# Seven-product pairs: the third output sum behind the last product, the low part behind a weight sum, and a fifth ordinary pair at the head of each module

## The chip, the cores and the metric

The kernel runs on one core of one Trainium2 chip. The metric is the device time of one execution in microseconds (us), the median of several runs. Engines are named as in the profile: PE (TensorE, matmuls), PEld (its weight loads), DVE (VectorE), ACT (ScalarE), POOL (GpSimd), SP (the queue that issues most transfers).

## What is computed

The reference is a trunk of two layers on 512 tokens of width 1024. Each layer is a mixer (a convolution module in layer 0, a chunked gated DeltaNet in layer 1) between two half-step feed-forward modules, with a shift, scale and gate from a conditioning vector. The change concerns the feed-forward modules of layer 1 alone:

```
gate, up = split(h @ w_in, 2)             # 1024 -> 2 x 2816
y = (silu(gate) * up) @ w_out             # 2816 -> 1024
x = x + 0.5 * (1 + mod) * y
```

## The kernel before, in words

All products are made of float32 values split into a high and a low part, and each product is three matmuls: high by high, high by low, low by high (`mm3`, lines 175 to 177, and the copy of it in `seven`, lines 661 to 663). The activations lie as feature tiles by 512 tokens: `hh` and `hl` for the input h, `ahi` and `alo` for silu(gate) * up.

`ffn` (line 501 on) handles the 2816 hidden features as 22 pairs; a pair is 128 features of gate and the same 128 of up. The pairs come in three groups of 7, 7 and 8 (`GROUPS`). After a group, its part of the second matrix product is added to x in eight parts of 128 output features, one block each. Below, a module is one of these feed-forward modules, of which layer 1 has two, and a block is one call of `block`.

An **ordinary pair** is two calls of `block`: 8 chunks of 128 input features, times three matmuls of 512 columns, for gate and again for up. Before them the raw weights are loaded (`raw`, three buffers), copied to the high part on ACT (`whi`) and subtracted on DVE (`wlo`): a weight split, made by `feed.prep`. Afterwards come `glu_a` (silu of gate, ACT), `glu_b` (times up, DVE line 552), and `glu_c` (the copy ahi on ACT, and alo on DVE).

A **seven-product pair** (`seven`) computes the same with seven products of half-size operands in place of eight, in the manner of Strassen: input features and tokens are cut in two, and each product is 4 chunks times three matmuls of 256 columns, 84 matmuls in all. It needs sums of the activations, `th` and `tl`, made once per module in four tasks (`sums_h`, with two additions on POOL, line 565, and six operations on DVE, lines 568 to 575), and sums of each pair's weights, made while the pair ahead of it runs (`sums_w`, four parts):

- `first`: s1 on POOL (line 594) from the raw up weights.
- `second`: the copy gh on ACT, s2 on DVE (line 602), the remainder gl on DVE, two copies of sums on ACT.
- `third`: s3 on POOL (line 612), a copy on ACT, s4 on DVE (line 617), three remainders on DVE (line 583), two copies on ACT.
- `fourth`: two remainders on DVE (line 583), and the next two raw loads.

The seven products go to three PSUM tiles Y, X and Z of one bank each. Products 0, 2, 4 and 6 add up in the left half of Y, products 1 and 5 in the left half of X, product 3 goes to the left half of Z. In between, ACT copies what has been summed so far: p1 after product 0 (line 674), p5 after product 1, u2 after product 2, u3 after product 4 (line 684). DVE makes three output sums from them: the left half of Z (line 680), the right half of Y from u3 and p5 (line 685), and the right half of Z (line 688). Then Z holds gate, and Y holds up. The silu is issued at the end of the pair; the product, ahi and alo are kept back in the list `late`, and `settle` issues them behind product 0 of the next pair.

`LEAD` says how many ordinary pairs stand at the head of a module, while the activation sums are made: four. In this head, `side` is a list of tasks of which each `block` issues one: the three remaining tasks of `sums_h`, then the four parts of the first `sums_w` in two tasks. Three of the first four outputs are begun by the stage ahead, so four ordinary pairs have five calls of `block`.

All of it stands under a manual schedule: each engine works off its instructions in the order in which the program issues them, and semaphores make an instruction wait for the tiles that it reads or overwrites. Two engines on one PSUM bank are kept apart in the same way.

Of the kernel before, what the change touches and what calls it, by code (L numbers as in the profile page):

```python
# [48 lines left out]
ARB = 3  # L49
PAD = (40, 168)  # L50
KQ = KT // 2
LEAD = {(1, 0): 4, (1, 1): 4}
SNW = 7
XP = ((0, 1), (1, 1), (2, 2), (4, 2), (6, 2))
WARM = (4, 7, 4)
# [54 lines left out]
def trunk_kernel(ctx: ExitStack, tc: tile.TileContext, x_in, c_in, vecs, consts, w_ada, w_st,  # L110
# [390 lines left out]
    def ffn(layer, which, nxt, first=None):  # L501
# [4 lines left out]
        with tc.tile_pool(name=nm("ffn"), bufs=1) as ap, ExitStack() as ax:  # L506
# [19 lines left out]
            box = {}  # L526
# [25 lines left out]
                dve.tensor_tensor(pr, box["s"], u, ALU.mult)  # L552

            def glu_c(jj):
                pr = box["pr"]
                act.copy(ahi[:, jj, :], pr)  # L556
                dve.tensor_tensor(alo[:, jj, :], pr, ahi[:, jj, :].bitcast(F32), ALU.subtract)  # L557

            def sums_h(th, tl):
                def task(k):  # L560
# [18 lines left out]
            def sums_w(box):  # L579
                st = {}  # L580

                def low(dst, src, hi):
                    dve.tensor_tensor(dst, src, hi.bitcast(F32), ALU.subtract)  # L583
# [12 lines left out]
                def second():  # L596
                    g, s1 = st["g"], st["s1"]
                    gh = wp.tile([P, KT, P], F32R, tag="whi", name=nm("whi"))
                    gl = wp.tile([P, KT, P], F32R, tag="wlo", name=nm("wlo"))
                    act.copy(gh, g)  # L600
                    st["s2"] = s2 = raw_s("sq")
                    dve.tensor_tensor(s2, s1, g[:, :KQ, :], ALU.subtract)
                    low(gl, g, gh)
                    st["h1"] = h1 = fresh("shi")
                    act.copy(h1[:, 0], s1)
                    act.copy(h1[:, 1], s2)
                    st["gw"] = gh, gl
# [34 lines left out]
            late = []  # L642

            def settle():
                while late:
                    late.pop(0)()

            def seven(w, th, tl, jj, prep):
                l, r = halves
                lo4, hi4 = slice(0, KQ), slice(KQ, KT)  # L650

                def T_(i):
                    return th[:, i], tl[:, i]

                def H_(ks, sl):
                    return hh[:, ks, sl], hl[:, ks, sl]

                def prod(i, ps, m, ends):
                    (whi, wlo), (mhi, mlo) = w[i], m
                    for k in range(KQ):  # L660
                        pe.matmul(ps, whi[:, k, :], mhi[:, k, :], start=ends in (0, 2) and k == 0, stop=False, skip_group_check=True)  # L661
                        pe.matmul(ps, whi[:, k, :], mlo[:, k, :], start=False, stop=False, skip_group_check=True)  # L662
                        pe.matmul(ps, wlo[:, k, :], mhi[:, k, :], start=False, stop=ends in (2, 3) and k == KQ - 1, skip_group_check=True)  # L663

                Y, X, Z = mm_tile(), mm_tile(), mm_tile()
                y, e = Y[:, l], X[:, l]
                pp = scratch("ssum").rearrange("p (a n) -> p a n", a=2)
                uu = scratch("t", bufs=2).rearrange("p (a n) -> p a n", a=2)
                p1, p5, u2, u3 = pp[:, 0], pp[:, 1], uu[:, 0], uu[:, 1]
                prod(0, y, H_(lo4, l), 0)  # L670
                settle()
                prep[0]()
                prod(1, e, T_(0), 0)
                act.copy(p1, y)
                prep[1]()
                prod(2, y, T_(1), 1)
                act.copy(p5, e)
                prod(3, Z[:, l], H_(hi4, l), 2)
                act.copy(u2, y)  # L679
                dve.tensor_tensor(Z[:, l], Z[:, l], p1, ALU.add)  # L680
                prep[2]()
                prod(4, y, T_(2), 1)
                prod(5, e, H_(hi4, r), 3)
                act.copy(u3, y)
                dve.tensor_tensor(Y[:, r], u3, p5, ALU.add)
                prep[3]()
                prod(6, y, T_(3), 3)
                dve.tensor_tensor(Z[:, r], e, u2, ALU.add)
                glu_a(Z)

                def rest():
                    glu_b(Y)
                    glu_c(jj)

                late.append(rest)

            def no():
                pass
# [1 line left out]
            for gi, n in enumerate(GROUPS):  # L700
                ahi = ap.tile([P, n, T], F32R, tag="ahi", name=nm("ahi"))
                alo = ap.tile([P, n, T], F32R, tag="alo", name=nm("alo"))
                if gi == 0 and lead < NPAIR:
                    th = ap.tile([P, 4, KQ, H2], F32R, tag="th", name=nm("th"))
                    tl = ap.tile([P, 4, KQ, H2], F32R, tag="tl", name=nm("tl"))
                    side += sums_h(th, tl)
                    side.pop(0)()
                    nxw = {}
                    s4 = sums_w(nxw)
                    side += [lambda: (s4[0](), s4[1]()), lambda: (s4[2](), s4[3]())]  # L710
                for jj in range(n):
                    if starts[gi] + jj >= lead:
                        w, nxw = nxw["w"], {}
                        if jj < n - 1:
                            prep = sums_w(nxw)
                        else:
                            prep = (no, feed.prep, feed.prep, feed.prep)
                        seven(w, th, tl, jj, prep)
                        continue
                    if len(begun) > 1:  # L720
# [7 lines left out]
                        step(rate[1])  # L728
                    glu_b(u)
                    glu_c(jj)  # L730
                settle()

                if gi == ng - 1:
# [1229 lines left out]
```

## Time and profile before

| | |
|---|---|
| runs shown | 2060.54, 2062.14, 2063.51 us (median 2062.14) |
| profiled execution, its own time | 2059.63 us |
| its span in the profile | 2057.8 us |
| busy: PE, PEld, DVE, ACT, POOL | 96%, 83%, 67%, 44%, 15% of the span |
| mean granted clock of TensorE | 0.984 |

The profile is of one execution. A row of the timeline gives start, length, engine, line of the kernel, operation, tiles written and read, and in brackets how long the engine had been idle and what ended that. A matmul's length includes its pass through the array, so the distance of two starts tells how long one occupies PE.

### The profile page before, as it was taken

Reading aid. Unit: us, or ns where it says so; the run is one execution under the profiler, and the core shown is the slowest. Engines: PE = TensorE matmul, PEld = TensorE weight load, DVE = VectorE, ACT = ScalarE, POOL = GpSimd, SP = SyncE. Lnnn points to the kernel's source line nnn. Section 1 sums busy time; section 2 is a strip of 40 time slices with the busy share of each in tenths; the row PEclk is TensorE's granted clock in tenths of the full one; section 3 lists DMA queues with packets and bytes.
Section 4 is the critical chain, followed back from the end, with each engine's and each line's share of the span. In section 5 each row is a group of like instructions: output and inputs, shape, how many; then the busy total and the mean of one; then the engine's idle time right before and its main releaser. Section 6 shows DMA issues by size and latency. Waiting matters only on the chain.

```text
span 2057.8 us, 29707 instructions
## 1 busy us (share of the span) xinstructions
PE 1982.2 (96%) x11651; PEld 1718.2 (83%) x11651; DVE 1373.2 (67%) x2190; ACT 904.7 (44%) x1660; POOL 317.5 (15%) x228
## 2 busy tenths in 40 slices
PE   8999999998899999999899999999899998999998
PEld 6888888877898888889889899887677897898997
DVE  7767676799865556546857576676745668475674
ACT  6422222564642222224535354476656545353452
POOL 0000000399100000001202020024210103021110
PEclk9999999999899999999999999999899999999999
DMA  8767776222235666532233333322111222333231
GB/s 301 236 226 236 229 235 225 98 82 84 90 117 188 209 190 208 162 95 72 81 101 96 103 95 122 110 77 72 62 54 41 64 91 81 94 103 113 83 113 62
DMA packets 78495, 262.29 MB, mean 127 GB/s; under 512 B 8337, under 2 KB 14097, under 8 KB 78226
## 3 DMA queue, kind: packets, MB, share of 16 engines
q1 hardware_dynamic: 77810, 259.87, 39.6%
q8 instruction: 91, 1.49, 0.3%
q10 hardware_dynamic: 544, 0.52, 0.1%
q14 instruction: 50, 0.41, 0.1%
HBM read 254.59 MB, written 5.77 MB: 127 GB/s over the span
## 4 chain that ended last, share of the span: by engine, by line
PE 77%; DVE 11%; ACT 4%; issue 4%; POOL 3%; DMA 1%; SPq 0%; DVEq 0%; POOLq 0%; ACTq 0%
PE mm L175 19%; PE mm L176 19%; PE mm L177 19%; PE mm L661 5%; PE mm L663 4%; PE mm L662 4%; POOL pacc L849 3%; DVE slo L583 2%; DVE sq L617 1%; DVE wlo L583 1%; PE mm L1616 1%; DVE x L1358 1%; PE mm L1638 1%; PE mm L1624 1%; PE aux L380 1%
## 5 line engine op out<-in xcount | busy, mean ns | idle before, releaser
L175 PE MATMUL mm<-hh,whi 128*128 128x512 f32 (+1 forms) x1392 | 518.9, 374 | 6.2 <-ACT hh L276 4.4
L176 PE MATMUL mm<-hl,whi 128*128 128x512 f32 (+1 forms) x1392 | 513.1, 369 | 1.6 <-DVE hl L280 1.3
L177 PE MATMUL mm<-hh,wlo 128*128 128x512 f32 (+1 forms) x1392 | 511.2, 368 | 1.8 <-DVE wlo L167 1.8
L167 DVE TENSOR_TENSOR wlo<-raw,whi 128x1024 fp32r<-128x1024 f32 (+1 forms) x219 | 267.8, 1224 | 156.3 <-ACT whi L166 152.1
L166 ACT CAST whi<-raw 128x1024 fp32r<-128x1024 f32 (+1 forms) x219 | 221.8, 1014 | 220.2 <-PE mm L176 195.3
L175 PEld LDWEIGHTS mm<-hh,whi 128*128 128x128 f32 x1392 | 263.4, 190 | 51.9 <-ACT hh L276 5.5
L177 PEld LDWEIGHTS mm<-hh,wlo 128*128 128x128 f32 x1392 | 264.2, 190 | 46.3 <-DVE wlo L167 2.9
L176 PEld LDWEIGHTS mm<-hl,whi 128*128 128x128 f32 x1392 | 264.4, 190 | 45.1 <-DVE hl L280 3.7
L175 PE MATMUL mm<-ahi,whi 128*128 128x512 f32 (+1 forms) x768 | 286.2, 373 | 0.0
L176 PE MATMUL mm<-alo,whi 128*128 128x512 f32 (+1 forms) x768 | 285.6, 372 | 0.0
L177 PE MATMUL mm<-ahi,wlo 128*128 128x512 f32 (+1 forms) x768 | 285.5, 372 | 0.0
L176 PEld LDWEIGHTS mm<-alo,whi 128*128 128x128 f32 x768 | 144.8, 189 | 24.9
L177 PEld LDWEIGHTS mm<-ahi,wlo 128*128 128x128 f32 x768 | 144.7, 188 | 24.9
L175 PEld LDWEIGHTS mm<-ahi,whi 128*128 128x128 f32 x768 | 144.7, 188 | 24.7
L429 DVE CUSTOM_DVE_ANT_0 ajunk<-araw,cs 128x1024 bf16<-128x1024 f32 x128 | 156.1, 1220 | 0.6
L556 ACT CAST ahi<-t 128x512 fp32r<-128x512 f32 x88 | 54.7, 622 | 223.7 <-DVE t L552 223.7
L548 ACT ACTIVATE sil<-mm 128x512 f32<-128x512 f32 x88 | 52.6, 598 | 214.3 <-PE mm L177 121.8
L473 DVE SCALAR_TENSOR_TENSOR x<-mm,gate,x 128x512 f32<-128x512 f32 x64 | 48.1, 751 | 122.8 <-PE mm L177 122.8
L661 PE MATMUL mm<-th,shi 128*128 128x256 f32 x432 | 124.3, 288 | 1.5 <-ACT t L679 1.3
L662 PE MATMUL mm<-tl,shi 128*128 128x256 f32 x432 | 123.7, 286 | 0.0
L663 PE MATMUL mm<-th,slo 128*128 128x256 f32 x432 | 123.6, 286 | 0.0
L557 DVE TENSOR_TENSOR alo<-t,ahi 128x512 fp32r<-128x512 f32 x88 | 76.9, 873 | 60.5 <-ACT ahi L556 60.5
(317 smaller groups left out, 3566.3 us busy)
## 6 DMA issues: line engine op xcount, KB each, us to landing
raw<-in_w_fi_dram SPq DMA_DIRECT2D x169, 512.0 KB, 3.6
araw<-in_w_ada_dram SPq DMA_DIRECT2D x128, 512.0 KB, 4.5
raw<-in_w_fo_dram SPq DMA_DIRECT2D x64, 448.0 KB, 3.4
raw<-in_w_dn_dram SPq DMA_DIRECT2D x33, 512.0 KB, 3.3
raw<-in_w_fo_dram SPq DMA_DIRECT2D x32, 512.0 KB, 3.6
stage<-in_w_ada_dram SPq DMA_DIRECT2D x16, 512.0 KB, 6.5
raw<-in_w_glu_dram SPq DMA_DIRECT2D x16, 512.0 KB, 3.6
raw<-in_w_pw_dram SPq DMA_DIRECT2D x8, 512.0 KB, 3.3
```

What stands on the lines that cost most here:

```text
L166: act.copy(whi[:, :nk, :], raw[:, :nk, :])
L167: dve.tensor_tensor(wlo[:, :nk, :], raw[:, :nk, :], whi[:, :nk, :].bitcast(F32), ALU.subtract)
L175: pe.matmul(ps, whi[:, k, :], mhi, start=first, stop=False)
L176: pe.matmul(ps, whi[:, k, :], mlo, start=False, stop=False)
L177: pe.matmul(ps, wlo[:, k, :], mhi, start=False, stop=last)
L429: dve.tensor_tensor_reduce(junk, raw, ada["cs"], 1.0, 0.0, ALU.mult, ALU.add, accum_out=mod[:, layer, col:col + 1])
L557: dve.tensor_tensor(alo[:, jj, :], pr, ahi[:, jj, :].bitcast(F32), ALU.subtract)
L583: dve.tensor_tensor(dst, src, hi.bitcast(F32), ALU.subtract)
L661: pe.matmul(ps, whi[:, k, :], mhi[:, k, :], start=ends in (0, 2) and k == 0, stop=False, skip_group_check=True)
L662: pe.matmul(ps, whi[:, k, :], mlo[:, k, :], start=False, stop=False, skip_group_check=True)
L663: pe.matmul(ps, wlo[:, k, :], mhi[:, k, :], start=False, stop=ends in (2, 3) and k == KQ - 1, skip_group_check=True)
L849: pool.tensor_tensor(pacc[m][:, c], pacc[m][:, c], pr[:, c], ALU.add)
```

## The change

It has four parts. The output sum of line 685 (right half of Y) is no longer issued between products 5 and 6 but with the product of silu and up, in `rest`, which `settle` issues behind product 0 of the next pair. The list `late` now has two entries per pair, and `settle` issues one at a time: alo, now `glu_d`, comes out behind the weight sum s2 of the next pair, or in the last pair of a group ahead of a weight split. Two scratch tiles are allocated after `settle` in place of before it. And `LEAD` is five, so pair 4 of each of the two modules is an ordinary pair; at the head, the four parts of the first `sums_w` are spread over four calls of `block`, the first of which issues none.

```diff
@@ -49,7 +49,7 @@
 ARB = 3
 PAD = (40, 168)
 KQ = KT // 2
-LEAD = {(1, 0): 4, (1, 1): 4}
+LEAD = {(1, 0): 5, (1, 1): 5}
 SNW = 7
 XP = ((0, 1), (1, 1), (2, 2), (4, 2), (6, 2))
 WARM = (4, 7, 4)
@@ -552,9 +552,10 @@
                 dve.tensor_tensor(pr, box["s"], u, ALU.mult)
 
             def glu_c(jj):
-                pr = box["pr"]
-                act.copy(ahi[:, jj, :], pr)
-                dve.tensor_tensor(alo[:, jj, :], pr, ahi[:, jj, :].bitcast(F32), ALU.subtract)
+                act.copy(ahi[:, jj, :], box["pr"])
+
+            def glu_d(jj):
+                dve.tensor_tensor(alo[:, jj, :], box["pr"], ahi[:, jj, :].bitcast(F32), ALU.subtract)
 
             def sums_h(th, tl):
                 def task(k):
@@ -600,6 +601,7 @@
                     act.copy(gh, g)
                     st["s2"] = s2 = raw_s("sq")
                     dve.tensor_tensor(s2, s1, g[:, :KQ, :], ALU.subtract)
+                    settle()
                     low(gl, g, gh)
                     st["h1"] = h1 = fresh("shi")
                     act.copy(h1[:, 0], s1)
@@ -642,7 +644,7 @@
             late = []
 
             def settle():
-                while late:
+                if late:
                     late.pop(0)()
 
             def seven(w, th, tl, jj, prep):
@@ -664,12 +666,12 @@
 
                 Y, X, Z = mm_tile(), mm_tile(), mm_tile()
                 y, e = Y[:, l], X[:, l]
+                prod(0, y, H_(lo4, l), 0)
+                settle()
+                prep[0]()
                 pp = scratch("ssum").rearrange("p (a n) -> p a n", a=2)
                 uu = scratch("t", bufs=2).rearrange("p (a n) -> p a n", a=2)
                 p1, p5, u2, u3 = pp[:, 0], pp[:, 1], uu[:, 0], uu[:, 1]
-                prod(0, y, H_(lo4, l), 0)
-                settle()
-                prep[0]()
                 prod(1, e, T_(0), 0)
                 act.copy(p1, y)
                 prep[1]()
@@ -682,17 +684,17 @@
                 prod(4, y, T_(2), 1)
                 prod(5, e, H_(hi4, r), 3)
                 act.copy(u3, y)
-                dve.tensor_tensor(Y[:, r], u3, p5, ALU.add)
                 prep[3]()
                 prod(6, y, T_(3), 3)
                 dve.tensor_tensor(Z[:, r], e, u2, ALU.add)
                 glu_a(Z)
 
                 def rest():
+                    dve.tensor_tensor(Y[:, r], u3, p5, ALU.add)
                     glu_b(Y)
                     glu_c(jj)
 
-                late.append(rest)
+                late.extend((rest, lambda: glu_d(jj)))
 
             def no():
                 pass
@@ -707,14 +709,14 @@
                     side.pop(0)()
                     nxw = {}
                     s4 = sums_w(nxw)
-                    side += [lambda: (s4[0](), s4[1]()), lambda: (s4[2](), s4[3]())]
+                    side += [no, lambda: (s4[0](), s4[1]()), s4[2], s4[3]]
                 for jj in range(n):
                     if starts[gi] + jj >= lead:
                         w, nxw = nxw["w"], {}
                         if jj < n - 1:
                             prep = sums_w(nxw)
                         else:
-                            prep = (no, feed.prep, feed.prep, feed.prep)
+                            prep = (no, lambda: (settle(), feed.prep()), feed.prep, feed.prep)
                         seven(w, th, tl, jj, prep)
                         continue
                     if len(begun) > 1:
@@ -728,6 +730,8 @@
                         step(rate[1])
                     glu_b(u)
                     glu_c(jj)
+                    glu_d(jj)
+                settle()
                 settle()
 
                 if gi == ng - 1:
```

What moves on the engines is shown at three places. First DVE, through one seven-product pair of the second group, from the left half of Z on (names: mm are the PSUM tiles, t holds u2 and u3 or the gate product, ssum p1 and p5, pr s1 or s3, sq s2 or s4, slo and wlo remainders). Before:

```order
L680 TENSOR_TENSOR mm_8669<-mm_8669,ssum_8670 128x256
L617 TENSOR_TENSOR sq_8744<-raw_8532,sq_8706 128x512
L583 TENSOR_TENSOR slo_8746<-pr_8688,shi_8709 128x512
L583 TENSOR_TENSOR slo_8746<-sq_8706,shi_8709 128x512
L583 TENSOR_TENSOR wlo_8742<-raw_8648,whi_8741 128x512
L685 TENSOR_TENSOR mm_8667<-t_8671,ssum_8670 128x256
L583 TENSOR_TENSOR slo_8779<-pr_8739,shi_8750 128x512
L583 TENSOR_TENSOR slo_8779<-sq_8744,shi_8750 128x512
L688 TENSOR_TENSOR mm_8669<-mm_8668,t_8671 128x256
L552 TENSOR_TENSOR t_8818<-sil_8799,mm_8667 128x512
L557 TENSOR_TENSOR alo_8536<-t_8818,ahi_8535 128x512
L602 TENSOR_TENSOR sq_8840<-pr_8822,raw_8650 128x512
```

In the changed kernel:

```order
L682 TENSOR_TENSOR mm_8602<-mm_8602,ssum_8621 128x256
L619 TENSOR_TENSOR sq_8678<-raw_8466,sq_8639 128x512
L584 TENSOR_TENSOR slo_8680<-pr_8619,shi_8643 128x512
L584 TENSOR_TENSOR slo_8680<-sq_8639,shi_8643 128x512
L584 TENSOR_TENSOR wlo_8676<-raw_8581,whi_8675 128x512
L584 TENSOR_TENSOR slo_8712<-pr_8673,shi_8684 128x512
L584 TENSOR_TENSOR slo_8712<-sq_8678,shi_8684 128x512
L689 TENSOR_TENSOR mm_8602<-mm_8601,t_8622 128x256
L693 TENSOR_TENSOR mm_8600<-t_8622,ssum_8621 128x256
L552 TENSOR_TENSOR t_8750<-sil_8732,mm_8600 128x512
L603 TENSOR_TENSOR sq_8773<-pr_8753,raw_8583 128x512
L558 TENSOR_TENSOR alo_8470<-t_8750,ahi_8469 128x512
```

The right half of Y (L685, now L693) went from between the remainders to behind the right half of Z, and alo went behind s2 (L602, now L603).

Second DVE at the head of the first module of layer 1, from the last remainder of the activation sums on. Before:

```order
L575 TENSOR_TENSOR tl_7651<-pr_7796,th_7650 128x2x256
L552 TENSOR_TENSOR t_7809<-sil_7768,mm_7770 128x512
L557 TENSOR_TENSOR alo_7649<-t_7809,ahi_7648 128x512
L602 TENSOR_TENSOR sq_7843<-pr_7838,raw_7646 128x512
L583 TENSOR_TENSOR wlo_7841<-raw_7646,whi_7840 128x1024
L617 TENSOR_TENSOR sq_7881<-raw_7646,sq_7843 128x512
L583 TENSOR_TENSOR slo_7883<-pr_7838,shi_7846 128x512
L583 TENSOR_TENSOR slo_7883<-sq_7843,shi_7846 128x512
L583 TENSOR_TENSOR wlo_7879<-raw_7678,whi_7878 128x512
L583 TENSOR_TENSOR slo_7890<-pr_7876,shi_7887 128x512
L583 TENSOR_TENSOR slo_7890<-sq_7881,shi_7887 128x512
```

In the changed kernel:

```order
L576 TENSOR_TENSOR tl_7651<-pr_7802,th_7650 128x2x256
L552 TENSOR_TENSOR t_7815<-sil_7768,mm_7776 128x512
L558 TENSOR_TENSOR alo_7649<-t_7815,ahi_7648 128x512
L167 TENSOR_TENSOR wlo_7820<-raw_7678,whi_7819 128x1024
L603 TENSOR_TENSOR sq_7882<-pr_7877,raw_7727 128x512
L584 TENSOR_TENSOR wlo_7880<-raw_7727,whi_7879 128x1024
L552 TENSOR_TENSOR t_7888<-sil_7850,mm_7852 128x512
L558 TENSOR_TENSOR alo_7649<-t_7888,ahi_7648 128x512
L619 TENSOR_TENSOR sq_7922<-raw_7727,sq_7882 128x512
L584 TENSOR_TENSOR slo_7924<-pr_7877,shi_7885 128x512
L584 TENSOR_TENSOR slo_7924<-sq_7882,shi_7885 128x512
L584 TENSOR_TENSOR wlo_7920<-raw_7774,whi_7919 128x512
```

One more weight split (L167) stands here, and another gate product with its alo has come between the weight sums of the first seven-product pair.

Third ACT at the same head, at the start of the first seven-product pair. Before:

```order
L623 CAST shi_7887<-pr_7876 128x512
L624 CAST shi_7887<-sq_7881 128x512
L556 CAST ahi_7648<-t_7897 128x512
L674 COPY ssum_7904<-mm_7901 128x256
L600 CAST whi_7933<-raw_7727 128x1024
L605 CAST shi_7939<-pr_7918 128x512
```

In the changed kernel:

```order
L617 CAST whi_7919<-raw_7774 128x512
L625 CAST shi_7928<-pr_7917 128x512
L626 CAST shi_7928<-sq_7922 128x512
L548 ACTIVATE sil_7931<-mm_7892 128x512
L555 CAST ahi_7648<-t_7965 128x512
L676 COPY ssum_7986<-mm_7969 128x256
L601 CAST whi_8001<-raw_7823 128x1024
```

The copy ahi of the last ordinary pair stands ahead of p1 (ssum) in both; a silu has come before it.

## Rows read from the trace of the kernel before

**Rows 1.** What PE waited for, whole span: total us, times, longest us.

```profile
PE mm L661 <- DVE mm L685: 10.9, 28, 0.4
...
PE mm L661 <- ACT whi L600: 5.4, 2, 2.7
...
PE mm L663 <- DVE wlo L583: 3.9, 2, 1.9
```

**Rows 2.** Timeline of PE, pairs 20 and 21 (the last of 0 to 21): start us, length, engine, line, tiles.

```profile
1247.89 0.28 PE L661 MATMUL mm<-hh,whi 128*128 128x256 f32 x1
...
1256.41 0.28 PE L663 MATMUL mm<-hh,slo 128*128 128x256 f32 x1
1257.08 0.39 PE L661 MATMUL mm<-th,whi 128*128 128x256 f32 x1 [0.39 <-DVE mm L685]
...
1258.61 0.28 PE L661 MATMUL mm<-hh,whi 128*128 128x256 f32 x1
...
1268.69 0.40 PE L175 MATMUL mm<-ahi,whi 128*128 128x512 f32 x1
```

**Rows 3.** Timeline of DVE in pair 20, one row for each step spoken of.

```profile
1247.41 0.42 DVE L688 TENSOR_TENSOR mm<-mm,t 128x256 f32<-128x256 f32 x1
1248.50 0.69 DVE L552 TENSOR_TENSOR t<-sil,mm 128x512 f32<-128x512 f32 x1 [0.66 <-ACT sil L548]
1249.88 1.14 DVE L557 TENSOR_TENSOR alo<-t,ahi 128x512 fp32r<-128x512 f32 x1 [0.69 <-ACT ahi L556]
...
1251.54 1.21 DVE L583 TENSOR_TENSOR wlo<-raw,whi 128x1024 fp32r<-128x1024 f32 x1
1253.85 0.43 DVE L680 TENSOR_TENSOR mm<-mm,ssum 128x256 f32<-128x256 f32 x1 [1.10 <-PE mm L663]
1254.19 0.68 DVE L617 TENSOR_TENSOR sq<-raw,sq 128x512 f32<-128x512 f32 x1
1254.79 0.69 DVE L583 TENSOR_TENSOR slo<-pr,shi 128x512 fp32r<-128x512 f32 x1
...
1256.60 0.43 DVE L685 TENSOR_TENSOR mm<-t,ssum 128x256 f32<-128x256 f32 x1
...
1258.14 0.43 DVE L688 TENSOR_TENSOR mm<-mm,t 128x256 f32<-128x256 f32 x1
```

**Rows 4.** Timeline of ACT in pair 20: ahi, p1 and u3.

```profile
1249.22 0.62 ACT L556 CAST ahi<-t 128x512 fp32r<-128x512 f32 x1 [0.75 <-DVE t L552]
1249.75 0.36 ACT L674 COPY ssum<-mm 128x256 f32<-128x256 f32 x1
...
1255.44 0.37 ACT L684 COPY t<-mm 128x256 f32<-128x256 f32 x1
```

**Rows 5.** Timeline of POOL in pair 20: s1 and s3.

```profile
1247.91 1.29 POOL L594 TENSOR_TENSOR pr<-raw 128x512 f32<-128x512 f32 x1 [8.03 <-DVE mm L688]
1249.16 1.30 POOL L612 TENSOR_TENSOR pr<-raw,raw 128x512 f32<-128x512 f32 x1
```

**Rows 6.** The page's row of weight loads: engine, operation, times, KB, median us to landing.

```profile
raw<-in_w_fi_dram SPq DMA_DIRECT2D x169, 512.0 KB, 3.6
```

**Rows 7.** Timeline of PE at the head of the first module.

```profile
987.67 0.39 PE L175 MATMUL mm<-hh,whi 128*128 128x512 f32 x1
...
992.88 0.39 PE L177 MATMUL mm<-hh,wlo 128*128 128x512 f32 x1
995.95 0.39 PE L661 MATMUL mm<-hh,whi 128*128 128x256 f32 x1 [2.68 <-ACT whi L600]
...
1012.15 0.28 PE L661 MATMUL mm<-hh,whi 128*128 128x256 f32 x1
```

**Rows 8.** Timeline of DVE at the same head: fourth activation sum, pair 2's product.

```profile
990.64 0.41 DVE L568 TENSOR_TENSOR pr<-sq 128x256 f32<-128x256 f32 x1
...
993.62 0.68 DVE L552 TENSOR_TENSOR t<-sil,mm 128x512 f32<-128x512 f32 x1
```

**Rows 9.** Two stretches: length, busy PE, PEld, DVE, ACT, POOL, granted clock, DMA.

```profile
990.00:1000.00 10.00, 5.38 (x24) 4.28 (x23) 9.05 (x14) 5.89 (x10) 3.04 (x3) 0.85 0.00 0
...
1435.00:1445.00 10.00, 8.64 (x41) 6.90 (x40) 9.55 (x21) 3.18 (x11) 0.43 (x1) 1.00 0.18 60
```

## The prediction

> **What bounds the kernel now.** I read the views in this order: PE's waits, PE's timeline across one pair, then DVE, ACT and POOL in the same stretch, then the head of a module. PE is the bound, so only its idle time can be won. In the list of PE's waits [rows 1] three lines belong to the code that the change touches: 28 waits of the first matmul of a product for the DVE sum of L685, and at two places a wait for a weight copy (2.7 us) and then for a weight remainder (1.9 us).
>
> The 28 waits are one per pair, always at one place. A seven-product pair is 84 matmuls of 256 columns. Pair 21 runs from 1258.61 to 1268.69, which is 10.08 us or 84 x 0.12, so nothing stops it; it is the last of its group. Pair 20 runs from 1247.89 to 1258.61, 10.72 us [rows 2]. Product 5 issues its last matmul at 1256.41, and product 6 begins at 1257.08 instead of 1256.53, named as waiting for L685. The gap and a longer first matmul make 0.64 us. DVE shows why [rows 3]: it starts L685 at 1256.60 because four weight sums and remainders (L617, L583 three times) stand between it and L680. Its two inputs were there before: ACT's copy u3 ran from 1255.44 to 1255.81 [rows 4]. Product 6 accumulates into the left half of Y and L685 writes the right half of the same bank, so one stands behind the other. All 28 are alike: 36 pairs, less six that end a group and less the first pair of each module.
>
> That first pair is a case of its own [rows 7]. The last ordinary matmul issues at 992.88, so the pair could begin at 993.11. It begins at 995.95, and pair 5 begins at 1012.15: 19.04 us for what takes 10.08. DVE was late: it begins the fourth task of activation sums at 990.64 and pair 2's product only at 993.62, though the blocks of pair 2 were over before the block that begins at 987.67, and all eight weight sums of the first seven-product pair still stand behind it [rows 8]. In this stretch the granted clock fell to 0.85 of full speed as a mean over 10 us, part of it at 1.2 instead of 2.4 GHz [rows 9].
>
> **The change, part by part.** (1) *The sum of L685 goes behind product 6.* Product 6 then waits only for u3, which ends 7.92 us after the pair's start (1255.81 less 1247.89), while the product is due at 8.64: 0.7 us to spare. 28 x 0.64 = **17.9 us** would go. What is late next? Counted from the pair's start, DVE's chain after product 3 starts L680 at 5.96. L688 stood 4.29 behind that (1253.85 to 1258.14) and now stands 3.96 behind, without L685's 0.33: at 9.92. From L688 to the gate product was 1.09, from there to the copy ahi 0.72, to p1 0.53, and p1 takes 0.36 [rows 3, 4]. So p1 ends at 12.62, which is 2.54 of the next pair. Product 2, which overwrites what p1 reads, is due at 2.88. It keeps 0.34 us, where it had 0.65. The moved sum waits for product 6 (ended 0.2 into the next pair) and runs from 0.2 to 0.6, in the time in which DVE waited 0.66 for the silu [rows 3]. It costs nothing as long as that wait stays.
>
> (2) *alo goes behind the weight sum s2.* DVE's work in a pair is 7.6 us by the distances in [rows 3]: nine steps of 0.60, three of 0.33 to 0.35, and gl with 1.21, besides what POOL holds up. s2 must now wait for POOL's s1, and s1 for a transfer. That transfer is released when s4 (L617) ends: 6.98 into a pair. In the pair ahead of 20 that was at 1244.15 (1254.87 less 10.72), and s1 started at 1247.91, 3.76 later; as a median of 169, such transfers land 3.6 us after their issue [rows 6]. So s1 starts at about 0.66 of the next pair. POOL follows at once with s3, and a DVE operation on two SBUF tiles that meets a POOL operation ends only after it: alo took 1.14 instead of 0.69, ending 0.56 behind s3 [rows 3, 5]. s2 now meets s3 in each pair and ends 3.1 behind the start of s1 (2.55 for the two, and 0.56), at about 3.8. alo 0.6 and gl 1.2 follow, to 5.6. L680 is due at 5.96: 0.3 to 0.4 us left, so I cost this at nothing.
>
> (3) *A fifth ordinary pair.* Its 48 matmuls of 512 columns take 0.2268 each (987.67 to 992.88 is 23 steps), 10.89 us, where a clean seven-product pair takes 10.08: the pair costs 0.81 us more, twice. But it stands in the place of the 19.04: 19.04 - 10.89 = 8.15, twice **16.3 us**, if the new head does not wait at all. For that DVE gets two more blocks. I follow it from 990.64. One more ordinary weight split (1.2, a remainder of gl's shape) goes ahead, so pair 2's product is at 994.8 and its alo would start at 996.2. POOL's s1 and s3, whose transfer lands some 3.8 us behind that split, stand at about 995.7 to 998.3 and hold alo and the last block's remainder wlo, which ends between 998.6 and 999.8. That block begins at 993.11 + 5.44 = 998.55 and wants wlo at its third matmul, 999.0: a wait of 0 to 0.8. Behind it DVE has s2 and gl (1.8), pair 3's product and alo with the wait for ahi (1.95), six sums and remainders (3.6), and pair 4's product; ACT's ahi and then p1 follow, to about 1008.6. The first seven-product pair begins at 1004.8, so its product 2, due at 1007.7, waits about 0.9. u2 stands behind another s2 that POOL holds, so product 4 waits about 1.1. Sum 2.8, and 0.1 for each restart: **3.1 us per module**. The bounds are 0 and the 9.0 us of today's head. I take 3.1, because DVE's queue gives it step by step. The clock stayed at 1.00 through single gaps of this size (PE busy 8.64 of 10 us at 1435, [rows 9]), so I add nothing for it.
>
> The order of PE, ACT and POOL in a pair does not change, and of the other stages only the numbering of lines. Two modules: 17.9 + 16.3 - 6.2 = **28.0 us** off. The profiled execution took 2059.6 us; the median of the runs shown is 2.5 above. On that median: 2062.1 - 28.0 = **2034 us**.
>
> **The rivals.** *The wait goes to product 2.* The moved sum stands on DVE just ahead of POOL's s1. If s1 got there first, the sum would wait for up to its whole 1.29 us, and the gate product, ahi and p1 behind it. It would start at 1.4 instead of 0.2, the product at 1.75 instead of 0.93, and p1 end at 3.35, so product 2 would wait 0.5, with the restart 0.6 per pair. For it speaks that alo, a DVE operation on two SBUF tiles, was held in this way. The Trainium skill (SBUF — State Buffer, "Who interferes with whom") states it for every DVE instruction with two SBUF inputs against a GpSimd instruction that reads SBUF, and lets the one that issues first hold the port; by that the moved sum, which reads u3 and p5 from SBUF, would be held too. No row of L685 meets POOL, so the trace leaves it open. Against it: s1 starts at about 0.66 and the sum at 0.2. Of the 17.9 us only 28 x 0.04 would be left, with the 10.1 of the head (16.3 - 6.2): 2051 us. Chance 0.08.
>
> *The head is no better than now.* The same late DVE queue, with 9.0 us lost per module and a slowed clock again. For it: DVE is 90% busy there [rows 9]. Against it: 10.9 more us for DVE, of which its added work takes 4. 2034 + 2 x 5.9 = 2046 us. Chance 0.08.
>
> *The sum still holds PE.* If the wait stayed where it is, only the head would win: 2062 - 10 = 2052 us. Against it: in the changed program product 6 waits for ACT alone. Chance 0.02.
>
> *The other side: the weights' loop becomes the bound.* Now that s2 stands early and DVE waits for it, a closed loop runs through each pair: end of s4, transfer (3.76), s1 and s3 (2.55), rest of s2 (0.55), alo (0.6), gl (1.2), L680 and s4 (1.0): 9.7 us. Below 10.08 it is hidden. It would eat all the gain at 10.72 + 10.1/28 = 11.08, so if transfers took 5.2 us; at 5.7 the loop is 11.6 and the kernel 28 x 0.88 - 10 = 15 slower, 2077 us. Against it: the median landing [rows 6], and a demand for bytes that rises only by the 6% by which a pair gets shorter. Chance 0.03.
>
> **How the numbers follow.** Forecast 0.79, the rivals 0.08, 0.08, 0.02 and 0.03. The forecast itself runs from 2027 (no wait at all at the heads, 6.2 less) to about 2040 (3 us more per head). The range leaves out the upper half of the second case and the rest: **2027 to 2042**. A difference under 0.2% (4 us) can hardly be told from none. Faster by more than that takes in the forecast, the first three rivals nearly whole, 0.95; the same 0.02; slower 0.03.
>
> **What would show it.** In the profile after, the waits of PE for the moved sum are gone, and pairs inside a group last 10.08. In DVE's timeline the sum stands between the last sum of Z (L688 before) and the gate product, starting 0.2 after the pair, and s2 takes about 1.7 us behind s1. At the head PE works through ten more us without a gap and then shows up to three waits of about 1 us: for wlo, for p1 and for u2, with the clock at 1.00. I am wrong if pairs last over 10.2, with PE waiting at product 2 for p1 or at product 4 for u2 in every pair; or if the first seven-product pair still shows a gap of several us and a fallen clock.

## Result and profile after

| | before | after |
|---|---|---|
| median of the compared runs (4 each) | 2061.72 us | 2031.36 us (2029.44 to 2033.11) |
| ratio, 95% interval | | 0.9852 [0.9835, 0.9869] |
| profiled execution / its span | 2059.63 / 2057.8 us | 2029.44 / 2027.6 us |
| mean granted clock | 0.984 | 0.989 |
| module 1, module 2 of layer 1 | 302.81, 302.79 us | 288.47, 288.77 us |
| everything else in the profiled execution's span | 1452.2 us | 1450.3 us |

About 30 us went, where 28.0 was forecast. A module's length runs here from the first matmul of its first call of `block` to the matmul that follows its last seven-product pair. Where module 1 begins before (its end is the last row of [rows 2]), then its start and end after:

```profile
965.88 0.40 PE L175 MATMUL mm<-hh,whi 128*128 128x512 f32 x1
```

```profile
963.59 0.40 PE L175 MATMUL mm<-hh,whi 128*128 128x512 f32 x1
...
1252.06 0.40 PE L175 MATMUL mm<-ahi,whi 128*128 128x512 f32 x1
```

The modules lost 14.3 and 14.0 us, 28.4 together. The other 1.9 us lie outside the changed code: module 1 begins 2.3 us earlier, and the stretches behind it are 0.4 us longer in all. Executions of one kernel differ there by as much.

The head of the page after, then three lines of what PE waited for over the whole span (total us, times, longest us):

```profile
span 2027.6 us, 29553 instructions
...
PE 1970.7 (97%) x11579; PEld 1708.4 (84%) x11579; DVE 1379.9 (68%) x2172; ACT 896.5 (44%) x1644; POOL 313.5 (15%) x224
```

```profile
PE mm L177 <- DVE wlo L167: 2.9, 4, 1.4
...
PE mm L663 <- ACT t L681: 1.8, 2, 0.9
...
PE mm L663 <- ACT ssum L676: 1.4, 2, 0.7
```

The 28 waits for the sum and the four long ones at the two heads [rows 1] are not in the list any more. What is left at each head is a wait for u2 (L681), one for p1 (L676) and one for a weight remainder of an ordinary block (4 times in the whole kernel for 2 before). The last two are new. The wait for u2 stood in the late first pair before, too:

```profile
PE mm L661 <- ACT t L679: 1.3, 2, 0.8
```

**A pair inside a group.** PE's timeline, from one pair's first matmul to the next one's (start us, length, engine, line, tiles):

```profile
1231.90 0.28 PE L663 MATMUL mm<-hh,whi 128*128 128x256 f32 x1
...
1241.98 0.28 PE L663 MATMUL mm<-hh,whi 128*128 128x256 f32 x1
```

That is 10.08 us where [rows 2] had 10.72. DVE, POOL and ACT in the same pair:

```profile
1231.73 0.43 DVE L689 TENSOR_TENSOR mm<-mm,t 128x256 f32<-128x256 f32 x1
1232.17 0.43 DVE L693 TENSOR_TENSOR mm<-t,ssum 128x256 f32<-128x256 f32 x1
1232.83 0.69 DVE L552 TENSOR_TENSOR t<-sil,mm 128x512 f32<-128x512 f32 x1 [0.22 <-ACT sil L548]
1233.95 1.77 DVE L603 TENSOR_TENSOR sq<-pr,raw 128x512 f32<-128x512 f32 x1 [0.43 <-POOL pr L595]
1235.64 0.68 DVE L558 TENSOR_TENSOR alo<-t,ahi 128x512 fp32r<-128x512 f32 x1
1236.25 1.21 DVE L584 TENSOR_TENSOR wlo<-raw,whi 128x1024 fp32r<-128x1024 f32 x1
1237.86 0.43 DVE L682 TENSOR_TENSOR mm<-mm,ssum 128x256 f32<-128x256 f32 x1 [0.41 <-PE mm L665]
```

```profile
1232.62 1.29 POOL L595 TENSOR_TENSOR pr<-raw 128x512 f32<-128x512 f32 x1 [7.51 <-DVE mm L693]
1233.88 1.29 POOL L614 TENSOR_TENSOR pr<-raw,raw 128x512 f32<-128x512 f32 x1
```

```profile
1233.55 0.62 ACT L555 CAST ahi<-t 128x512 fp32r<-128x512 f32 x1 [0.75 <-DVE t L552]
1234.08 0.36 ACT L676 COPY ssum<-mm 128x256 f32<-128x256 f32 x1
```

The moved sum (L693) starts 0.27 into the pair. The wait for the silu behind it has shrunk from 0.66 [rows 3] to 0.22. s2 (L603) is now the operation that meets POOL's s3 and takes 1.77, and alo is back to 0.68. L682 still waits 0.41 for PE (0.21 to 0.50 in the 22 pairs that follow another in their group and are not its last): that is what is left before DVE becomes late. p1 (L676) ends at 1234.44, which is 2.54 into the pair; product 2 is due at 2.88. The row of s1 names L693 as what ended its wait, but in seven of the 22 pairs s1 began up to 0.08 before that sum had ended, so it does not wait for it; in experiment 5 the same row names the transfer.

**The head.** PE's waits in module 1, then DVE and POOL behind them:

```profile
997.29 0.50 PE L177 MATMUL mm<-hh,wlo 128*128 128x512 f32 x1 [0.42 <-DVE wlo L167]
1006.14 0.39 PE L663 MATMUL mm<-th,shi 128*128 128x256 f32 x1 [0.70 <-ACT ssum L676]
1010.17 0.39 PE L663 MATMUL mm<-th,shi 128*128 128x256 f32 x1 [0.90 <-ACT t L681]
```

```profile
994.91 2.32 DVE L167 TENSOR_TENSOR wlo<-raw,whi 128x1024 fp32r<-128x1024 f32 x1
...
1004.48 0.68 DVE L552 TENSOR_TENSOR t<-sil,mm 128x512 f32<-128x512 f32 x1
1005.85 1.36 DVE L558 TENSOR_TENSOR alo<-t,ahi 128x512 fp32r<-128x512 f32 x1 [0.69 <-ACT ahi L555]
1007.13 1.79 DVE L603 TENSOR_TENSOR sq<-pr,raw 128x512 f32<-128x512 f32 x1
```

```profile
994.40 1.74 POOL L614 TENSOR_TENSOR pr<-raw,raw 128x512 f32<-128x512 f32 x1
1005.38 1.28 POOL L595 TENSOR_TENSOR pr<-raw 128x512 f32<-128x512 f32 x1 [9.24 <-DMA raw<-in_w_fi_dram]
1006.61 1.76 POOL L614 TENSOR_TENSOR pr<-raw,raw 128x512 f32<-128x512 f32 x1
```

The wait for wlo leads back to the remainder of 2.32 us, where its shape takes 1.2: it stood beside POOL's s3. The wait for u2 leads back to alo and s2 (1.36 and 1.79, for 0.7), which met POOL as well, since u2 stands on ACT behind the copy of s2. The wait for p1 comes from DVE's queue as a whole: the last ordinary pair's gate product is reached only at 1004.48, and ahi and p1 follow it on ACT. The first seven-product pair lasts 12.17 us, 12.22 in module 2. The clock stayed up (length, busy PE, PEld, DVE, ACT, POOL, granted clock, DMA):

```profile
990.00:1000.00 10.00, 9.58 (x43) 7.61 (x42) 8.62 (x11) 5.68 (x9) 3.00 (x2) 1.00 0.33 98
1000.00:1010.00 10.00, 8.58 (x60) 7.74 (x58) 9.06 (x12) 5.79 (x12) 2.99 (x2) 1.00 0.36 107
```

Before, the stretch from 990 to 1000 had 5.38 us of PE and a clock of 0.85 [rows 9].

### The profile page after: what moved, and what is told of

The parts are those of the page before. It is cut to its first block, busy times and chain, and to the rows that moved or that the text cites. A ratio compares the mean times of both kernels' runs of the same rounds, so it can differ in the third digit from the quotient of the medians.

```text
span 2027.6 us, 29553 instructions
## 1 busy us (share of the span) xinstructions
PE 1970.7 (97%) x11579; PEld 1708.4 (84%) x11579; DVE 1379.9 (68%) x2172; ACT 896.5 (44%) x1644; POOL 313.5 (15%) x224
## 4 chain that ended last, share of the span: by engine, by line
PE 82%; DVE 7%; ACT 4%; POOL 3%; issue 2%; DMA 0%; SPq 0%; DVEq 0%; POOLq 0%; ACTq 0%
PE mm L175 19%; PE mm L176 19%; PE mm L177 19%; PE mm L663 5%; PE mm L665 5%; PE mm L664 5%; POOL pacc L853 3%; PE mm L1620 1%; PE mm L1642 1%; DVE x L1362 1%; PE mm L1628 1%; PE mm L1851 1%; PE aux L380 1%; PE mm L1852 1%; PE mm L1855 1%
## 5 line engine op out<-in xcount | busy, mean ns | idle before, releaser
L175 PE MATMUL mm<-hh,whi 128*128 128x512 f32 (+1 forms) x1424 | 530.3, 374 | 6.2 <-ACT hh L276 4.4
L176 PE MATMUL mm<-hl,whi 128*128 128x512 f32 (+1 forms) x1424 | 524.6, 369 | 1.6 <-DVE hl L280 1.3
L177 PE MATMUL mm<-hh,wlo 128*128 128x512 f32 (+1 forms) x1424 | 523.0, 368 | 2.9 <-DVE wlo L167 2.9
L167 DVE TENSOR_TENSOR wlo<-raw,whi 128x1024 fp32r<-128x1024 f32 (+1 forms) x223 | 274.8, 1234 | 160.8 <-ACT whi L166 156.9
L175 PEld LDWEIGHTS mm<-hh,whi 128*128 128x128 f32 x1424 | 268.9, 190 | 53.4 <-ACT hh L276 5.5
L177 PEld LDWEIGHTS mm<-hh,wlo 128*128 128x128 f32 x1424 | 269.6, 189 | 49.4 <-DVE wlo L167 4.9
L663 PE MATMUL mm<-th,shi 128*128 128x256 f32 x408 | 115.9, 284 | 3.2 <-ACT t L681 1.8
L665 PE MATMUL mm<-th,slo 128*128 128x256 f32 x408 | 115.4, 283 | 0.0
L664 PE MATMUL mm<-tl,shi 128*128 128x256 f32 x408 | 115.4, 283 | 0.0
L595 POOL TENSOR_TENSOR pr<-raw 128x512 f32<-128x512 f32 x34 | 47.1, 1386 | 403.3 <-DMA raw<-in_w_fi_dram 225.8
```

The costliest lines, as they stand in the source:

```text
L167: dve.tensor_tensor(wlo[:, :nk, :], raw[:, :nk, :], whi[:, :nk, :].bitcast(F32), ALU.subtract)
L175: pe.matmul(ps, whi[:, k, :], mhi, start=first, stop=False)
L176: pe.matmul(ps, whi[:, k, :], mlo, start=False, stop=False)
L177: pe.matmul(ps, wlo[:, k, :], mhi, start=False, stop=last)
```

## Experiments

The theory: the sum held product 6, the head was DVE's lateness, the two gains add, and the moved sum goes free because it begins ahead of POOL's s1. The main rivals: the sum's wait moves to product 2 (POOL holds it), or the head is not better. Since executions scatter outside the modules, each kernel is read by the length of its two modules as well as by its time.

**1. The sum alone**, in the kernel before:

```diff
-                dve.tensor_tensor(Y[:, r], u3, p5, ALU.add)
 ...
                 def rest():
+                    dve.tensor_tensor(Y[:, r], u3, p5, ALU.add)
```

(with the scratch tiles allocated behind `settle`, as in the change)

> The kernel before with one edit: the sum of L685 behind product 6. Four ordinary pairs and the order of alo as before. Theory: the 28 waits of 0.64 us are due to this sum's place alone, so pairs inside a group take 10.08 and 17.9 us go: 2061.7 - 17.9 = about 2044, with the head as late as before (first seven-product pair 16 us and a gap of 2.7 before it). Rival: alo must be out of the way too, since s2, and behind it the copies u2 on ACT, come late without that; then PE waits at product 4 in each pair, 10.2 to 10.4 a pair, and 2048 to 2053.

Measured: 2051.66 us, ratio 0.9952 [0.9935, 0.9969]; modules 295.31 and 295.17, so 7.5 and 7.6 less, where the 14 waits of a module are worth 9.0. The waits for the sum are gone, and one for p1 has come in pair 5 of each module. PE's waits in this kernel, the one for u2 in the first seven-product pair, as before, and the new one:

```profile
PE mm L661 <- ACT t L679: 1.6, 2, 1.0
PE mm L661 <- ACT ssum L674: 1.1, 2, 0.6
```

Pair 5 waits for p1 at product 2 and lasts 10.89 us, since DVE is still behind from the head. With alo still behind ahi some pairs last 10.1 to 10.25, with the time lost at product 4, for u2, and the others 10.08: 0.6 to 0.7 us per module. So the median lies where the rival had put it, but what the rival names happens only in some pairs and is a small part of it. A second set of runs was to say whether the time above the sum of the modules was chance:

> The moved sum alone once more. Its two modules took 295.3 and 295.2 us, 15.1 less than before in all, which gives 2046; two of its five runs took that, three took 2052. Theory: the modules repeat (295 us each) and the 6 us are of other stages, where the granted clock falls for longer in some executions: the profile shows modules of 295 whatever the whole time is. Rival: the modules themselves take 298 in the longer executions, since the cover of 0.1 us at product 4 is used up.

Measured: 2046.69 us, 0.9939 [0.9922, 0.9957], modules 294.91 and 294.94. In both sets the executions lie either at 2043.5 to 2046.2 or at 2049.2 to 2053.9, the longer ones at a lower mean clock (0.981 and 0.982 against 0.984 to 0.987). Both profiles are of short executions, and their modules agree within 0.4 us: by them the moved sum is worth 15.1 to 15.8 us, where the medians say 9 and 15. No long execution of this kernel was profiled, so that its modules are no longer is not shown here; experiment 4 shows it for its kernel.

The second profile also says what set the pace of the late head. The first seven-product pairs of its two modules (length, busy PE, PEld, DVE, ACT, POOL, granted clock, DMA):

```profile
994.53:1010.54 16.01, 13.19 (x84) 12.48 (x85) 15.08 (x21) 8.81 (x18) 3.08 (x3) 0.79 0.35 103
1720.45:1736.55 16.10, 12.26 (x84) 11.65 (x85) 15.17 (x21) 8.81 (x18) 3.08 (x3) 0.89 0.35 101
```

The clock was higher in the second, and the pair no shorter; DVE was busy for 94% of both. So the fallen clock of [rows 9] was not what made this pair long.

**2. The head alone**: before, with five ordinary pairs and the new list of tasks.

```diff
-LEAD = {(1, 0): 4, (1, 1): 4}
+LEAD = {(1, 0): 5, (1, 1): 5}
 ...
-                    side += [lambda: (s4[0](), s4[1]()), lambda: (s4[2](), s4[3]())]
+                    side += [no, lambda: (s4[0](), s4[1]()), s4[2], s4[3]]
```

> The kernel before with one edit: five ordinary pairs, and the first weight sums over four calls of the block. The sum of L685 between products 5 and 6 as before. Theory: the head gains 16.3 - 6.2 = 10.1 us and the waits of 0.64 stay: about 2051, PE waiting for the sum 28 times again (a little less in the first pair of a module). Rival: the head's gain depends on the moved sum too, because DVE is short there; then the first seven-product pair shows waits of more than 2 us in all and the time stays above 2055.

Measured: 2049.25 us, 0.9946 [0.9929, 0.9962]; modules 297.04 and 297.13, so 5.8 and 5.7 less. Its PE waits keep the line of the sum, less pair 5 of each module, which is now the first seven-product pair:

```profile
PE mm L661 <- DVE mm L685: 10.1, 26, 0.4
```

The two parts by themselves make 13.3 per module, and together 14.2. Three things lie between, as far as the rows tell: the 0.8 that pair 5 loses in the first experiment does not arise where it is the first seven-product pair, the waits for u2 go with alo's new place, which neither experiment has, and pair 5's wait of 0.64 for the sum is counted in both. So the gains add, to within 1 us per module.

**3. alo back behind ahi**, in the changed kernel:

```diff
                     glu_c(jj)
+                    glu_d(jj)
 ...
-                late.extend((rest, lambda: glu_d(jj)))
+                late.append(rest)
```

> The changed kernel with alo again directly behind ahi; the moved sum and five ordinary pairs stay. Theory: alo's place gives only room: s2 would end 0.6 later, u2 with it, and product 4 would keep about 0.1 us in place of 0.7, so the time stays at 2031 within 1.5 us. Rival: alo's place is needed; PE waits at product 4 in each pair inside a group for 0.1 to 0.3 us, 2034 to 2040.

Measured: 2031.61 us, 0.986 [0.9845, 0.9875]; modules 289.15 and 288.93, 0.7 and 0.2 longer than in the changed kernel. Some pairs last 10.1 to 10.3, where all last 10.08 in the changed kernel: 0.5 and 0.3 us per module. The time goes at product 4, for u2. In one such pair, u2 and the two matmuls at the start of product 4, which was due at 1099.68:

```profile
1099.32 0.38 ACT L681 COPY t<-mm 128x256 f32<-128x256 f32 x1
...
1099.56 0.28 PE L665 MATMUL mm<-hh,wlo 128*128 128x256 f32 x1
1099.75 0.39 PE L663 MATMUL mm<-th,shi 128*128 128x256 f32 x1
```

alo's new place gives slack and a few tenths of a microsecond per module, not more.

**4. Six ordinary pairs**, with the weight sums two blocks later and no ordinary split taken once they have begun:

```diff
-LEAD = {(1, 0): 5, (1, 1): 5}
+LEAD = {(1, 0): 6, (1, 1): 6}
 ...
-                    side += [no, lambda: (s4[0](), s4[1]()), s4[2], s4[3]]
+                    side += [no, no, no, lambda: (s4[0](), s4[1](), stop.append(1)), s4[2], s4[3]]
```

(`block` leaves out `feed.prep` while `stop` holds something; the first seven-product pair empties it)

> The changed kernel with six ordinary pairs (the weight splits of the second matrix wait until the seven-product pair has begun). Theory: the head's remaining waits (0.76 for a remainder and 2.1 in the first seven-product pair) are DVE's backlog of some 2 us, which 10.9 more us clear; the sixth pair costs 0.81: 2 x (2.85 - 0.81) = 4.1 us less, 2027. Rival: the waits belong to the first seven-product pair wherever it stands (its weight sums are made in a hurry): then 2 x 0.81 more, 2033.

> Six ordinary pairs once more, beside five. Theory: its modules take 286.5 us, 2.2 less than with five, so 4.4 us less in all: about 2027 beside 2031. Rival: the gain is lost elsewhere, and the two cannot be told apart.

Measured: 2028.26 us, 0.985 [0.9827, 0.9873], and 2031.67 us, 0.9864 [0.9843, 0.9886]. The modules are 286.49 and 286.46 in the first profile, 286.51 and 286.46 in the second: 2.0 and 2.3 less than in the changed kernel. No wait is left at the head; the stretches of the second profile:

```profile
990.00:1000.00 10.00, 10.00 (x46) 8.29 (x45) 8.47 (x13) 4.28 (x8) 0.00 (x0) 1.00 0.28 77
1000.00:1010.00 10.00, 10.00 (x46) 8.29 (x45) 5.78 (x6) 5.20 (x8) 2.54 (x2) 1.00 0.41 127
1010.00:1020.00 10.00, 10.00 (x68) 9.22 (x67) 6.42 (x10) 5.01 (x10) 0.00 (x0) 1.00 0.38 100
```

So the head's waits are worth 2.8 to 3.1 us per module, and a sixth ordinary pair takes them for its 0.81. In whole executions the 4.3 us can't be told from the changed kernel: five of the eight runs lie at 2026.5 to 2030, and three at 2034.9 to 2036.1 with a clock of 0.983 to 0.985. The first profile is of one of these three, and it shows the loss outside the modules (1461.0 us, against 1452.6 in the second). Much of it is one stretch, first in the long execution, then in the other:

```profile
1500.00:1510.00 10.00, 10.00 (x49) 8.48 (x48) 2.09 (x9) 2.17 (x6) 0.94 (x1) 0.60 0.00 0
```

```profile
1500.00:1510.00 10.00, 10.00 (x69) 8.60 (x68) 4.02 (x16) 3.71 (x12) 0.73 (x1) 1.00 0.00 0
```

PE is busy throughout in both, at a granted clock of 0.60 in one and of 1.00 in the other, and gets 49 matmuls done in place of 69.

**5. The sum made to meet s1**: one more DVE product, into the X that nobody reads any more, ahead of the moved sum.

```diff
                 def rest():
+                    dve.tensor_tensor(X, box["s"], Z, ALU.mult)
                     dve.tensor_tensor(Y[:, r], u3, p5, ALU.add)
```

> The changed kernel with one more DVE operation ahead of the moved sum in each seven-product pair: silu times the silu's input, written over X, whose content is no longer used. It waits for the silu, so the moved sum starts about 1.5 us into the next pair, in the middle of POOL's s1. If a DVE operation with two SBUF inputs and a PSUM output is held by a POOL operation, the sum's row is 0.8 us long or more, p1 comes about 1.1 late, and a module takes 303 to 305 us, 2060 in all. If it is not held, the row keeps 0.43, product 2 waits 0.75 in each pair, and a module takes 298 to 300, about 2051.

Measured: 2062.59 us, 1.0015 [1.0005, 1.0025], no faster than before; modules 304.01 and 304.08. PE's waits; the line of the sum (its durations in ns, smallest, median, largest); the sum in DVE's timeline, and the s1 that it meets:

```profile
PE mm L663 <- ACT ssum L676: 24.9, 28, 1.1
```

```profile
L694 DVE TENSOR_TENSOR mm<-t,ssum x34: 426/730/894, 1019.8 to 2009.0; 128x256 f32<-128x256 f32 x34
```

```profile
1205.83 0.74 DVE L694 TENSOR_TENSOR mm<-t,ssum 128x256 f32<-128x256 f32 x1
...
1204.98 1.29 POOL L595 TENSOR_TENSOR pr<-raw 128x512 f32<-128x512 f32 x1 [8.55 <-DMA raw<-in_w_fi_dram]
```

In the changed kernel the same line reads:

```profile
L693 DVE TENSOR_TENSOR mm<-t,ssum x34: 432/433/434, 1014.9 to 1971.6; 128x256 f32<-128x256 f32 x34
```

The sum, which takes 0.43 in every pair of the changed kernel, took 0.73 here as a median of all 34, and 0.58 to 0.89 (median 0.78) in the 22 pairs where it met s1, about as expected. At 1205.83 it started inside s1 (1204.98 to 1206.27) and ended 0.30 after it. So the mechanism of the first rival exists, also for a sum that writes to PSUM. The rule of the Trainium skill (SBUF — State Buffer, "Who interferes with whom") that the prediction weighed agrees with this row.

The 31 us over the changed kernel are not its price alone, because the added product by itself puts the sum 1.3 us later. The run holds its own comparison. In the last pair of the second or third group POOL has no s1 to make, and the sum of the pair before it, issued at the same place (1.53 into the pair), keeps its 0.43. The sum there, and PE's wait for p1:

```profile
1262.25 0.43 DVE L694 TENSOR_TENSOR mm<-t,ssum 128x256 f32<-128x256 f32 x1
...
1264.38 0.39 PE L663 MATMUL mm<-th,shi 128*128 128x256 f32 x1 [0.61 <-ACT ssum L676]
```

These four pairs last 10.95 us. In the 22 pairs whose sum met s1, the sum ended 0.28 to 0.30 after s1 each time, PE waited 0.77 to 1.08, and the pair lasted 11.3 as a mean. So of the 1.2 us per pair the later place costs 0.87, and the hold 0.34. (The other two of the 28 waits are those of the heads.)

**6. gl computed twice** in each seven-product pair:

```diff
+                    if twice[0]:
+                        low(gl, g, gh)
                     low(gl, g, gh)
```

(`twice[0]` is set only where a seven-product pair issues the second part of the next one's weight sums)

> The changed kernel with the remainder gl computed twice in each seven-product pair that prepares another: 1.15 us more of DVE work between s2 and the left half of Z. Theory: the cover there is 0.3 to 0.4 us, and the loop of transfer, s1, s3, s2, alo, gl and s4 becomes the bound: pairs of 10.7 to 10.9 us, PE waiting for ACT at products 2 and 6, a module 296 to 299 us, 2047 to 2052. Rival: DVE had more room than the rows say (it is busy 7.6 of 10.08 us), pairs stay at 10.1 to 10.2 and the time within 3 us of 2031.

Measured: 2050.14 us, 0.9953 [0.9937, 0.997]; modules 297.51 and 297.34. Pairs in the middle of a group last mostly 10.75 to 10.97, with PE's new waits for u3:

```profile
PE mm L666 <- ACT t L691: 1.9, 10, 0.2
```

and a longer stretch at product 2. 1.26 us more DVE work (two remainders take 2.47, one 1.21) cost about 0.8 in such a pair, so about 0.4 was covered: the 0.41 that L682 waits in the changed kernel.

**7. The old list of tasks** with five ordinary pairs:

```diff
-                    side += [no, lambda: (s4[0](), s4[1]()), s4[2], s4[3]]
+                    side += [lambda: (s4[0](), s4[1]()), lambda: (s4[2](), s4[3]())]
```

> The changed kernel with the first weight sums of a module in two calls of the block, as before, in place of four with one left empty; five ordinary pairs stay. Theory: the head is short of DVE time, not of places in the order, so only where the waits fall changes: a module 288 to 289 us, 2031. Rival: the spread is what makes the head work; without it the first seven-product pair waits 2 us more, a module 290 to 292 and the time 2035 to 2039.

Measured: 2031.69 us, 0.9857 [0.9845, 0.987]; modules 288.01 and 288.08, 0.5 to 0.7 shorter than with the new list. PE's waits at the head:

```profile
1000.47 0.50 PE L177 MATMUL mm<-hh,wlo 128*128 128x512 f32 x1 [0.62 <-DVE wlo L167]
1009.80 0.39 PE L663 MATMUL mm<-th,shi 128*128 128x256 f32 x1 [1.14 <-ACT ssum L676]
```

There is a longer wait for p1 and none for u2; the first seven-product pair lasts 11.47 and 11.67, where it lasts 12.17 and 12.22 with the new list. The spread list is not what the head gains from; it rather costs half a microsecond.

**8. The changed kernel again**, for the scatter:

> The changed kernel once more, on one chip with the next three. In the first profiles each module (from its first ordinary block to the end of its last seven-product pair) took 302.8 us before and 288.5 and 288.8 after. Theory: these two lengths repeat within 0.5 us and the spread of whole executions comes from the other stages. Rival: the modules themselves vary by some us from run to run. Expected 2031.

Measured: 2032.11 us, 0.9867 [0.9852, 0.9881]; modules 288.49 and 288.81, within 0.04 of the first profile. The two profiles with six ordinary pairs agree within 0.03 as well, but those of the sum alone differ by 0.40 and 0.23. So modules do not vary by some us in any of these profiles, and a difference of 0.2 to 0.4 between two kernels is no more than one kernel shows. That leaves the 0.5 to 0.7 of experiment 7 just clear of it; in experiment 3 it is the lengths of the pairs that show the effect.

## Why the prediction held

**The sum (17.9 us).** Right. All 28 waits went and pairs last 10.08. The sum alone gave 15.1 to 15.8, and what was short of 17.9 is named: pair 5's wait for p1 (0.8 per module), which the fifth ordinary pair removes, and small waits for u2 (0.5 to 0.7), which alo's new place removes. The prediction had put the whole 17.9 down to the sum's place and costed alo's move at nothing. That it costs nothing was right, but the last 0.3 to 0.5 us per module of the 17.9 need it (experiment 3).

**What is late next.** p1 was to end 2.54 into the next pair, and does. s2 was to take about 1.7 behind s1 (1.77), the sum to start at 0.2 (0.27), L680 to keep 0.3 to 0.4 (0.41). Experiment 6 agrees with this last number.

**The head (16.3 less 3.1 per module).** Right in size and in its parts. With the 14 waits (9.0) and the shorter head (8.15) taken off the 302.8, 2.8 and 3.1 us per module are left to the new waits, of 0.42 (0.66 in module 2), 0.70 and 0.90 before restarts: for wlo, p1 and u2, as forecast. The steps came where DVE's queue had put them, counted from a module that begins 2.3 us earlier: wlo ends at 997.23, or 999.5 on the old count (forecast 998.6 to 999.8), and p1 at 1006.09, or 1008.4 (1008.6). The clock did not fall in either module. Experiment 4 takes these waits away, and the module gets shorter by 2.0 and 2.3, where 3.1 less 0.81 was to be had.

**The rivals.** The first was real as a mechanism and did not decide here. In the 22 pairs where both occur the sum began 0.35 to 0.65 us before s1, where the prediction had counted on 0.46. Experiment 5 shows what it costs to be on the other side of that: 0.34 us per pair for the hold, besides the later place. Experiment 2 excludes the second (a head no better) and experiment 1 the third (the sum still holds PE). The fourth, the closed loop through transfers, did not come about: landings stay at 3.6 us as a median, and in all 22 pairs L682 still waits for PE and not PE for it.

**What it did not forecast** are the last 2 us: 28.0 against 28.4 by modules, and 30.4 by medians. They lie outside the modules and are of the size of the scatter there. What sets that scatter, 8 to 10 us between the shortest and the longest run in experiments 1 and 4, was not tried and stays open; where it was profiled, it went with a granted clock that fell in one execution and not in another (experiment 4).

## What to carry to other kernels

Where the schedule keeps two engines apart on one PSUM bank, an operation on that bank holds up the matmuls behind it even when their data is ready, here 0.64 us in 28 pairs. Put it where the bank changes hands anyway, and count first what then becomes late, from each engine's queue, in tenths of a microsecond. When a stage starts late because its operands are still being made, give that time to a plain variant of the work until its waits cost less than the plain variant does: by the length of the module the sixth ordinary pair still paid, 2.0 to 2.3 us, though whole executions do not show it. And read a change of a few microseconds from the length of the stage that it touches: here that repeats within 0.4 us, and mostly within 0.04, while whole executions scatter by several.

## What the runs showed of the hardware

A DVE sum of two SBUF tiles into PSUM is held by a POOL operation as one into SBUF is: 0.43 us alone, 0.58 to 0.89 where s1 is running (experiment 5). The added product of experiment 5 reads one SBUF and one PSUM tile and kept 0.70 in all 34 rows, though it overlaps s1 too (1205.22 to 1205.92 beside 1204.98 to 1206.27).

The hold works both ways, which the prediction had not counted. s3 on POOL took 1.74 and 1.76 us at the head instead of 1.29; both times alo was still running on DVE when s3 began. In the 26 pairs where s3 had begun first and s2 came to it, s3 kept 1.29 to 1.31 and s2 took 1.77. So in these rows it is the operation that begins second that pays.
